# A hybrid attention, convolution and PEER layer: another layout of the gate matrix in memory, five row buffers, and three moved steps

## The chip, the cores and the metric

The kernel runs on one core of a Trainium2 chip, in one launch. The metric is the device time of that core in microseconds, taken as the median of several executions. The core has four engines that compute: TensorE (PE, with its weight loads shown as PEld), VectorE (DVE), ScalarE (ACT) and GpSimd (POOL). SyncE (SP) issues most of the DMAs, ACT and POOL issue some, and each engine works through its own instructions in the order in which they were laid down.

## The reference

One decoder layer on 512 tokens of width 1024. The first half (projections, sparse attention, convolution, output projection) ends at about 360 us and is not touched. The second half is a PEER layer over 16,384 single-neuron experts, with 8 heads that pick 16 experts each:

```
q = (hf @ w_q).reshape(T, PEER_HEADS, 2, 128)
s = einsum('thcd,hcnd->thcn', q, sub_keys)
s1, i1 = top_k(s[:, :, 0], 16);  s2, i2 = top_k(s[:, :, 1], 16)
cand = s1[..., :, None] + s2[..., None, :]        # 256 candidates a head
top_s, pos = top_k(cand, 16);  e_idx = take(cand_idx, pos);  gw = softmax(top_s)
act = gelu(einsum('td,thkd->thk', hc, u_tab[e_idx]))
out = einsum('thk,thkd->td', gw * act, v_tab[e_idx])
```

The result is scaled by a vector and added to the first half's output.

## The kernel before, in words

For the first 384 tokens (TD) the kernel does not gather rows: it multiplies them with all experts, in 128 tiles (NTILE) of 128 experts. The last 128 tokens are done by gathers instead: POOL fetches a U or V row for each token and pick (256 steps in all), and DVE multiplies and sums them.

**U tiles.** `u_split(i)` (line 1056) makes sure that the rows of the next tiles are on their way (`ld()`, line 1051, 512 KB each, four buffers shared by U and V rows), casts tile i to a high part on ACT and takes the low part on DVE. `u_mm` runs 24 matmuls of 384 columns (lines 1070 to 1072), and `u_evac` applies Gelu on ACT. The first eight tiles stay on chip, later ones are written to a spill area by a DMA that ACT issues, until V has begun.

**Routing.** The loop that ends at line 1044 projects one head after another; picking the best 16 is DVE's work and is put in a queue, of which `run(9.0)` takes a part per head. The candidates of each group of 128 tokens follow later, in the loop from line 1206.

**Gate matrix.** `w_chunk` and `w_mm` build, for 16 tokens at a time, the dense matrix of gate weights over all experts: comparisons on DVE, 64 short matmuls on PE, copies on ACT. Each of the 24 blocks of 16 tokens is written to a matrix `wd` in memory by a DMA that ACT issues at line 1138, 1 MB each. V reads it back in groups of eight expert tiles (`w_load`, line 1233; 1.5 MB, issued by SP, 17 loads).

**V tiles.** `v_prep(n)` (line 1286) loads the gate group where a new one begins, loads V rows ahead (line 1301), multiplies gates and Gelu outputs into `g` on DVE, and splits rows and `g` into high and low parts. `v_mm` runs 18 matmuls of 512 columns (lines 1326 to 1328). From about 915 to 1240 us one U tile and one V tile alternate, after that V runs alone. Gather steps are set between the tiles in a fixed proportion.

**Order.** A planner orders PE, ACT, SP and POOL by program order and readiness; from line 1194 on DVE's instructions run in the order of the program. So a DVE step that waits holds all that are written behind it. SP and ACT issue their DMAs in their one instruction stream too: where an issue is held, everything behind it waits.

Of the kernel before, what the change touches and what calls it, by code (L numbers as in the profile page):

```python
# [9 lines left out]
F32 = mybir.dt.float32  # L10
# [10 lines left out]
P = 128  # L21
S = 512
D = 1024
NT = S // P
ND = D // P
H = 8
NCMP = 32
HK = 128
NTILE = 128
TD = 384  # L30
# [78 lines left out]
def layer(ctx: ExitStack, tc: tile.TileContext, a, out):  # L109
    nc = tc.nc  # L110
    mult, add, sub = ALU.mult, ALU.add, ALU.subtract

    def tt(o, i0, i1, op):
        return nc.vector.tensor_tensor(out=o, in0=i0, in1=i1, op=op)  # L114
# [4 lines left out]
    def split(pool_hi, pool_lo, src, shape, tag, bufs=1):  # L119
        hi = pool_hi.tile(shape, F32R, name=tag + "hi", bufs=bufs)  # L120
        lo = pool_lo.tile(shape, F32R, name=tag + "lo", bufs=bufs)
        nc.scalar.copy(hi, src)  # L122
        tt(lo, src, hi.bitcast(F32), sub)
        return hi, lo

    const = ctx.enter_context(tc.tile_pool(name="const", bufs=1, side="left"))
    dram = ctx.enter_context(tc.tile_pool(name="dram", bufs=1, space=DRAM))
    x1d = dram.tile([S, D], F32, name="x1d")
    wd = dram.tile([P, TD // 16, NTILE, 16], F32, name="wd")

    cst = const.tile([P, C_N], F32, name="cst")
    ident = cst[:, C_ID:C_ID + P]
# [12 lines left out]
    with ExitStack() as pre:  # L145
# [630 lines left out]
        for i in range(N + 2):  # L776
            n, pr = i // 4, i % 4
# [132 lines left out]
        gw3 = h2p.tile([P, H, 16], F32, name="gw3")  # L910
        e_i = h2p.tile([P, HK], I32, name="e_i")

        ua = ctx.enter_context(tc.tile_pool(name="upA", bufs=1, side="left"))
        rp = rt.enter_context(tc.tile_pool(name="rpool", bufs=1, side="left"))
# [10 lines left out]
        def run(budget):  # L925
            used = 0.0
            while dq and used < budget:
                cost, f = dq.pop(0)
                f()
                used += cost  # L930
            return used
# [9 lines left out]
        def route_head(t, h, sc):  # L941
            for c in range(2):
                top16(vals[t][:, c, h, :], idxs[t][:, c, h, :], sc[:, t % 2, c, :], P, "s2")
# [5 lines left out]
        def route_items(t):  # L949
# [50 lines left out]
            def soft_b():  # L1000
# [6 lines left out]
            return [(1.6, cands)] + [(0.8, lambda h=h: top(h)) for h in range(H)] + \  # L1007
                [(0.5, soft_a), (2.0, decode), (3.6, lambda: look(0)), (3.6, lambda: look(1)), (0.8, soft_b)]

        wqp = rt0.enter_context(tc.tile_pool(name="wqp", bufs=1, side="right"))  # L1010
        w = wx
        nw[0] = 1
        for h in range(H):
            hi, lo = w
            if h + 1 < H:
                w = wload(a["wq"][h + 1], wqp)
            qs = []
            ps2 = [psQ.tile([P, S], F32, name="mm") for _ in range(2)]
            NS = 2 if h == 0 else 1
            for m in range(NS):  # L1020
                ms_ = slice(m * S // NS, (m + 1) * S // NS)
                for c in range(2):
                    wc = slice(c * P, (c + 1) * P)
                    for d in range(ND):
                        nc.tensor.matmul(ps2[c][:, ms_], hi[:, d, wc], h2hi[:, d, ms_], start=d == 0, stop=False)  # L1025
                        nc.tensor.matmul(ps2[c][:, ms_], hi[:, d, wc], h2lo[:, d, ms_], start=False, stop=False)  # L1026
                        nc.tensor.matmul(ps2[c][:, ms_], lo[:, d, wc], h2hi[:, d, ms_], start=False, stop=d == ND - 1)  # L1027
            for c in range(2):
                ps = ps2[c]
                q = wqk.tile([P, S], F32, name="qs", bufs=2)  # L1030
                nc.scalar.copy(q, ps)
                qs.append(q)
            for t2 in range(2):
                ps = psR.tile([P, 2, 2, P], F32, name="sc")
                for k in range(2):
                    t = 2 * t2 + k
                    for c in range(2):
                        nc.tensor.matmul(ps[:, k, c, :], qs[c][:, t * P:(t + 1) * P], kt[:, 2 * h + c, :],
                                         start=True, stop=True)
                sc = rp.tile([P, 2, 2, P], F32, name="scs", bufs=4)  # L1040
                nc.scalar.copy(sc, ps)
                dq.append((2.2, lambda t=2 * t2, h=h, sc=sc: route_head(t, h, sc)))
                dq.append((2.2, lambda t=2 * t2 + 1, h=h, sc=sc: route_head(t, h, sc)))
            run(9.0)

    up_ = ctx.enter_context(tc.tile_pool(name="upool", bufs=1, side="right"))
    acts = {}
    spill = dram.tile([P, NTILE, TD], F32, name="spill")
    RING = 8

    def ld():
        return ua.tile([P, D], F32, name="ld", bufs=4)

    ust, usp, ue, PU, UB = [], [], [], 2, 3

    def u_split(i):
        if i >= NTILE or i < len(usp):
            return
        while len(ust) < min(i + PU + 1, NTILE):
            ust.append(ld())  # L1060
            nc.sync.dma_start(ust[-1], a["uT"][len(ust) - 1].rearrange("p d e -> p (d e)"))
        src = ust[i].rearrange("p (d e) -> p d e", d=ND)
        usp.append(split(ua, ua, src, [P, ND, P], "u", bufs=UB))

    def u_mm(i, spilled=False):
        u_split(i)
# [21 lines left out]
    flat = lambda z: z.rearrange("p h k -> p (h k)")  # L1088
# [37 lines left out]
    def w_mm(c, q, e1, e2):  # L1126
        if q == 0:
            wbs[c] = wb_.tile([P, NTILE, 16], F32, name="wb", bufs=2)
        wb = wbs[c]
        for g in range(G):  # L1130
            ps = psQ.tile([P, 4, P], F32, name="mm")
            for j in range(4):
                nc.tensor.matmul(ps[:, j, :], e2[:, 4 * g + j, :], e1[:, 0, 2 * g + j // 2, :, j % 2], start=True, stop=False)
                nc.tensor.matmul(ps[:, j, :], e2[:, 4 * g + j, :], e1[:, 1, 2 * g + j // 2, :, j % 2], start=False, stop=True)  # L1134
            tl = q * CH + 4 * g
            act(wb[:, :, tl:tl + 4].rearrange("p i t -> p t i"), ps, AF.Copy, scale=1.0 / GW_SCALE)
        if q == 16 // CH - 1:
            nc.scalar.dma_start(wd[:, c], wb)

    def lists3():  # L1140
        ef = rp.tile([P, HK], F32, name="ef3")
        nc.vector.scalar_tensor_tensor(ef, flat(isel[3][:, 0]), 128.0, flat(isel[3][:, 1]), op0=mult, op1=add)
        nc.vector.tensor_copy(e_i, ef)
        gather_on.append(True)
# [3 lines left out]
    GB, PG = 16, 3  # L1148
# [18 lines left out]
    def gather_step(n):  # L1167
        kind, k = seq[n]
        g = gath(n)
        if kind == "u":  # L1170
            nc.vector.scalar_tensor_tensor(g, g, 1.0, h2n, op0=mult, op1=mult, accum_out=actg[:, k:k + 1])  # L1171
            if k % GB == GB - 1:
                bs = slice(k + 1 - GB, k + 1)
                act(actg[:, bs], actg[:, bs], AF.Gelu)
                tt(actg[:, bs], actg[:, bs], flat(gw3)[:, bs], mult)
        elif k == 0:
            nc.vector.tensor_scalar(acc, g, actg[:, 0:1], None, op0=mult)
        else:
            nc.vector.scalar_tensor_tensor(acc, g, actg[:, k:k + 1], acc, op0=mult, op1=add)  # L1179
# [19 lines left out]
            f()  # L1199
            bud += p - c  # L1200

    for i in range(UB - 1):
        u_split(i)
    while items or pend:
        bud += lead - 1.14
        todo, pend[:] = list(pend), []
# [19 lines left out]
    def group_load(held, k, name, src):  # L1226
        if k not in held:
            held[k] = vp.tile(list(src.shape), F32, name=name, bufs=2)
            nc.sync.dma_start(held[k], src)
            for j in list(held)[:-2]:  # L1230
                del held[j]

    def w_load(k):
        group_load(wts, k, "wt", wd[:, :, k * 8:k * 8 + 8, :])

    def s_load(k):
        group_load(sps, k, "sp", spill[:, k * 4:k * 4 + 4, :])
# [48 lines left out]
    def v_prep(n):  # L1286
        if n >= NTILE:
            return
        i = order[n]
        if n == 0 or i // 8 != order[n - 1] // 8:  # L1290
            w_load(i // 8)
            wseq.pop(0)
        wt = wts[i // 8]
        if i in acts:
            ac = acts.pop(i)
        else:
            if i % 4 == 0:
                s_load(i // 4)
                sseq.pop(0)
            ac = sps[i // 4][:, i % 4, :]  # L1300
        while len(vst) < min(n + 2, NTILE):
            m = order[len(vst)]
            vst.append(ld())
            nc.sync.dma_start(vst[-1], a["vn"][m * P:(m + 1) * P, :])
        if i % 4 == 2 and wseq:
            w_load(wseq[0])
        if i % 4 == 0 and sseq and n + 12 >= order.index(sseq[0] * 4):
            s_load(sseq[0])
        g = vp.tile([P, TD], F32, name="g", bufs=2)
        tt(g.rearrange("p (c t) -> p c t", t=16), wt[:, :, i % 8, :], ac.rearrange("p (c t) -> p c t", t=16), mult)  # L1310
        if n >= NTILE - KL + 2:
            v = split(ua, ua, vst[n].rearrange("p (d e) -> p d e", d=ND), [P, ND, P], "u", bufs=UB)
            v = tuple(z.rearrange("p d e -> p (d e)") for z in v)
        else:
            v = split(vp, vp, vst[n], [P, D], "v", bufs=2)
        gs = split(vp, vp, g, [P, TD], "gs", bufs=KL)
        vsp[n] = gs + v
# [62 lines left out]
```

## Time and profile before

| | |
|---|---|
| three runs | 1612.42, 1619.84, 1621.44 us; median 1619.84 |
| profiled execution | 1614.99 us; span from first to last instruction 1613.2 us |
| PE busy | 1560.4 us (97%) |
| DVE busy | 1293.1 us (80%) |
| ACT busy | 755.2 us (47%) |
| DMA | 416.31 MB, mean 258 GB/s |
| reads of `wd` by SP | 17 of 1536 KB |
| writes of `wd` by ACT | 24 of 1024 KB |
| rows of U, of V | 128 and 128 loads of 512 KB |

Busy shares are means over stages with different limits, so the stages are looked at one by one: U tiles beside routing (461 to 650 us), U tiles beside the gate matrix (650 to 900), U and V in turn (915 to 1225), V alone (to about 1600). The granted clock of TensorE stands in each row of a stretch as a share of full speed: 1.00 is 2.4 GHz, 0.50 is 1.2 GHz.

### The profile page before, as it was taken

The numbers are of one execution on the slowest core, as the hardware profiler recorded it, in microseconds if no ns is written. First come the engines' busy times: TensorE is split into PE (matmuls) and PEld (weight loads), VectorE is DVE, ScalarE is ACT, GpSimd is POOL, SyncE is SP. The second block draws the span as 40 slices with busy tenths as digits, with TensorE's granted clock in tenths as the row PEclk, the third lists the DMA queues.
The fourth block names the chain that finished last, engine by engine and source line by source line (L and its number), as shares of the span: only waits on it lengthen the run. The fifth ranks groups of instructions, "written<-read, shape, count | busy, mean of one in ns | idle before, by whom it ended". The sixth has DMA issues, their size and how long they took to land.

```text
span 1613.2 us, 24117 instructions
## 1 busy us (share of the span) xinstructions
PE 1560.4 (97%) x9033; PEld 1361.8 (84%) x9033; DVE 1293.1 (80%) x2590; ACT 755.2 (47%) x1234; POOL 323.3 (20%) x266
## 2 busy tenths in 40 slices
PE   5999998999999999999999999998999999999998
PEld 3779766898889999999999899997897888888887
DVE  4698667578989999988888387786788888878887
ACT  4335558634334544778778433233232333333332
POOL 0000000000002232221222044443454322222210
PEclk9999999999999999999999999999999999999999
DMA  8443242244006877888888989998999999999993
GB/s 316 151 154 123 107 155 79 95 159 152 15 27 206 297 256 252 308 321 311 314 317 283 336 323 337 328 320 312 347 320 346 340 352 352 359 344 350 350 366 143
DMA packets 157166, 416.31 MB, mean 258 GB/s; under 512 B 13036, under 2 KB 76268, under 8 KB 147960
## 3 DMA queue, kind: packets, MB, share of 16 engines
q1 hardware_dynamic: 104048, 236.73, 42.1%
q0 software_dynamic: 36864, 134.23, 23.2%
q10 hardware_dynamic: 16136, 43.79, 7.2%
q8 instruction: 71, 1.16, 0.3%
q14 instruction: 47, 0.39, 0.1%
HBM read 368.25 MB, written 45.88 MB: 257 GB/s over the span
## 4 chain that ended last, share of the span: by engine, by line
PE 71%; DVE 16%; DMA 6%; ACT 4%; issue 3%; SPq 0%; ACTq 0%; DVEq 0%
PE va L1327 8%; PE va L1328 8%; PE va L1326 8%; PE u L1070 7%; PE u L1071 7%; PE u L1072 7%; DVE acc L1179 3%; DVE ulo L114 3%; DVE ldg L1171 3%; DMA ld<-in_uT_dram 3%; DMA ld<-in_vn_dram 2%; ACT vhi L122 2%; PE mm L1026 2%; PE mm L1025 2%; PE mm L1027 2%
## 5 line engine op out<-in xcount | busy, mean ns | idle before, releaser
L1070 PE MATMUL u<-h2hi,uhi 128*128 128x384 f32 x1024 | 350.4, 342 | 7.4 <-ACT act L117 7.2
L1072 PE MATMUL u<-h2hi,ulo 128*128 128x384 f32 x1024 | 346.4, 338 | 4.4 <-DVE ulo L114 4.4
L1071 PE MATMUL u<-h2lo,uhi 128*128 128x384 f32 x1024 | 348.4, 340 | 0.0
L1163 POOL DMA_INDIRECT ldg<-in_un_dram,e_i x128 | 159.8, 1248 | 869.4 <-DVE cand L114 504.6
L1326 PE MATMUL va<-vhi,gshi 128*128 128x512 f32 x756 | 295.9, 392 | 5.3 <-ACT gshi L122 3.4
L1327 PE MATMUL va<-vlo,gshi 128*128 128x512 f32 x756 | 296.7, 393 | 1.6 <-DVE vlo L114 1.5
L1328 PE MATMUL va<-vhi,gslo 128*128 128x512 f32 x756 | 296.4, 392 | 0.0
L114 DVE TENSOR_TENSOR vlo<-ld,vhi 128x1024 fp32r<-128x1024 f32 x126 | 154.3, 1224 | 128.0 <-ACT vhi L122 127.9
L122 ACT CAST vhi<-ld 128x1024 fp32r<-128x1024 f32 x126 | 132.3, 1051 | 229.6 <-issue 164.6
L1163 POOL DMA_INDIRECT ldg<-in_vn_dram,e_i x128 | 161.3, 1260 | 362.8 <-DVE acc L1179 321.6
L1070 PEld LDWEIGHTS u<-h2hi,uhi 128*128 128x128 f32 x1024 | 194.5, 190 | 10.4 <-ACT act L117 8.3
L122 ACT CAST uhi<-ld 128x1024 fp32r<-128x1024 f32 x130 | 137.7, 1060 | 133.4 <-PE u L1071 86.2
L1072 PEld LDWEIGHTS u<-h2hi,ulo 128*128 128x128 f32 x1024 | 194.2, 190 | 5.0 <-DVE ulo L114 5.0
L1071 PEld LDWEIGHTS u<-h2lo,uhi 128*128 128x128 f32 x1024 | 194.5, 190 | 1.3
L114 DVE TENSOR_TENSOR ulo<-ld,uhi 128x1024 fp32r<-128x1024 f32 x130 | 158.5, 1221 | 27.7 <-ACT uhi L122 26.3
L1326 PEld LDWEIGHTS va<-vhi,gshi 128*128 128x128 f32 x756 | 142.8, 189 | 35.6 <-ACT gshi L122 3.7
L1327 PEld LDWEIGHTS va<-vlo,gshi 128*128 128x128 f32 x756 | 142.7, 189 | 31.9 <-DVE vlo L114 3.0
L1328 PEld LDWEIGHTS va<-vhi,gslo 128*128 128x128 f32 x756 | 142.7, 189 | 30.7 <-DVE gslo L114 0.9
L1179 DVE SCALAR_TENSOR_TENSOR acc<-ldg,actg,acc 128x1024 f32<-128x1024 f32 x127 | 162.5, 1279 | 0.0
L1171 DVE SCALAR_TENSOR_TENSOR ldg<-ldg,h2n 128x1024 f32<-128x1024 f32 x128 | 155.9, 1218 | 0.0
L122 ACT CAST gshi<-g 128x384 fp32r<-128x384 f32 x128 | 65.1, 509 | 156.7 <-DVE g L114 156.6
L117 ACT ACTIVATE wb<-mm 128x512 f32<-128x512 f32 x96 | 96.1, 1110 | 47.2 <-PE mm L1134 47.1
(317 smaller groups left out, 2502.8 us busy)
## 6 DMA issues: line engine op xcount, KB each, us to landing
ld<-in_uT_dram SPq DMA_DIRECT2D x128, 512.0 KB
ld<-in_vn_dram SPq DMA_DIRECT2D x128, 512.0 KB
wt<-wd SPq DMA_DIRECT2D x17, 1536.0 KB
wst<-in_wada_dram SPq DMA_DIRECT2D x24, 1024.0 KB
wd<-wb ACTq DMA_DIRECT2D x24, 1024.0 KB
spill<-actw ACTq DMA_DIRECT2D x84, 192.0 KB
sp<-spill SPq DMA_DIRECT2D x21, 768.0 KB
wst<-in_win_dram SPq DMA_DIRECT2D x9, 1024.0 KB
```

The source lines that it names most:

```text
L114: return nc.vector.tensor_tensor(out=o, in0=i0, in1=i1, op=op)
L117: return nc.scalar.activation(o, i, f, **k)
L122: nc.scalar.copy(hi, src)
L1070: nc.tensor.matmul(ps, hi[:, d, :], h2hi[:, d, :TD], start=d == 0, stop=False)
L1071: nc.tensor.matmul(ps, hi[:, d, :], h2lo[:, d, :TD], start=False, stop=False)
L1072: nc.tensor.matmul(ps, lo[:, d, :], h2hi[:, d, :TD], start=False, stop=d == ND - 1)
L1163: nc.gpsimd.indirect_dma_start(out=gst[-1], out_offset=None, in_=a["un" if kind == "u" else "vn"], in_offset=bass.IndirectOffsetOnAxis(ap= ...
L1171: nc.vector.scalar_tensor_tensor(g, g, 1.0, h2n, op0=mult, op1=mult, accum_out=actg[:, k:k + 1])
L1179: nc.vector.scalar_tensor_tensor(acc, g, actg[:, k:k + 1], acc, op0=mult, op1=add)
L1326: nc.tensor.matmul(vac[t][k], ghi[:, ts_], vhi[:, ks], start=f, stop=False)
L1327: nc.tensor.matmul(vac[t][k], ghi[:, ts_], vlo[:, ks], start=False, stop=False)
L1328: nc.tensor.matmul(vac[t][k], glo[:, ts_], vhi[:, ks], start=False, stop=l)
```

## The change

The matrix `wd` in memory gets another order of its axes: per partition first the 16 groups of eight expert tiles, then the 24 blocks of 16 tokens. Writing a block now puts 16 pieces of 512 bytes per partition at 16 places, where it was one piece of 8 KB; reading a group takes one piece of 12 KB per partition, where it was 24 pieces of 512 bytes. The row buffers are five, and V rows are asked for three ahead of the tile in work, where it was two. The first two `u_split` calls stand inside the loop over heads, in the last head ahead of `run(9.0)`. The product of Gelu outputs and gates of a batch of 16 gathers is moved from the end of the batch's last U step to the start of its first V step, one U step later. The index row of the gathers uses the tile `tmp` of the decode.

```
-    wd = dram.tile([P, TD // 16, NTILE, 16], F32, name="wd")
+    wd = dram.tile([P, NTILE // 8, TD // 16, 8, 16], F32, name="wd")
...
+            return ua.tile([P, D], F32, name="ld", bufs=5)
...
+            if h == H - 1:
+                for i in range(UB - 1):
+                    u_split(i)
             run(9.0)
...
-        return ua.tile([P, D], F32, name="ld", bufs=4)
...
-            nc.scalar.dma_start(wd[:, c], wb)
+            nc.scalar.dma_start(wd[:, :, c], wb.rearrange("p (k i) t -> p k i t", i=8))
...
-        ef = rp.tile([P, HK], F32, name="ef3")
+        ef = flat(rp.tile([P, H, 16], F32, name="tmp"))
...
                 act(actg[:, bs], actg[:, bs], AF.Gelu)
-                tt(actg[:, bs], actg[:, bs], flat(gw3)[:, bs], mult)
-        elif k == 0:
+            return
+        if k % GB == 0:
+            bs = slice(k, k + GB)
+            tt(actg[:, bs], actg[:, bs], flat(gw3)[:, bs], mult)
+        if k == 0:
...
-    for i in range(UB - 1):
-        u_split(i)
...
-        group_load(wts, k, "wt", wd[:, :, k * 8:k * 8 + 8, :])
+        group_load(wts, k, "wt", wd[:, k])
...
-        while len(vst) < min(n + 2, NTILE):
+        while len(vst) < min(n + 3, NTILE):
```

## Rows read from the trace of the kernel before

**Rows 1.** Stretches: us, busy (instructions) PE, PEld, DVE, ACT, POOL, PEclk, DMA, GB/s.
```profile
650.00:900.00 250.00, 249.97 (x1905) 235.24 (x1904) 221.25 (x290) 198.04 (x238) 52.28 (x36) 1.00 0.87 311
...
899.10:911.50 12.40, 12.40 (x73) 12.40 (x73) 3.68 (x3) 4.43 (x6) 0.00 (x0) 1.00 0.84 289
...
918.00:924.80 6.80, 5.49 (x12) 3.94 (x13) 2.16 (x3) 4.59 (x7) 0.00 (x0) 0.50 1.10 338
...
1095.50:1102.30 6.80, 4.35 (x14) 4.35 (x15) 2.18 (x3) 3.63 (x5) 0.00 (x0) 0.50 0.77 308
...
1100.00:1200.00 100.00, 99.19 (x496) 90.09 (x496) 82.20 (x103) 32.86 (x48) 45.14 (x35) 0.99 0.92 322
...
1235.40:1238.80 3.40, 3.40 (x9) 2.64 (x9) 3.40 (x5) 0.51 (x1) 1.93 (x2) 0.50 1.02 406
1240.00:1560.00 320.00, 320.00 (x1413) 264.94 (x1413) 262.93 (x352) 116.16 (x161) 82.64 (x79) 1.00 0.99 351
```

**Rows 2.** Waits of PE, 900 to 1240: us in total, times, longest us.
```profile
PE u L1070 <- ACT act L117: 6.2, 2, 5.3
PE va L1326 <- ACT gshi L122: 3.4, 1, 3.4
PE va L1326 <- ACT vhi L122: 1.9, 2, 1.5
PE va L1327 <- DVE vlo L114: 1.5, 2, 0.8
```

**Rows 3.** Timeline of SP: start us, us, what, times [idle before <-releaser].
```profile
904.62 0.62 SPq L1229 DMA_DIRECT2D wt<-wd  x1
905.36 3.58 SPq L1061 DMA_DIRECT2D ld<-in_uT_dram  x1
...
1076.85 0.53 SPq L1229 DMA_DIRECT2D wt<-wd  x1
1077.99 10.69 SPq L1061 DMA_DIRECT2D ld<-in_uT_dram  x1
...
1557.27 4.88 SPq L1304 DMA_DIRECT2D ld<-in_vn_dram  x2
```

**Rows 4.** Timeline of ACT and of DVE, where they waited between 900 and 1240.
```profile
917.74 1.04 ACT L122 CAST vhi<-ld 128x1024 fp32r<-128x1024 f32 x1 [8.86 <-DMA ld<-in_vn_dram]
...
1096.46 1.04 ACT L122 CAST uhi<-ld 128x1024 fp32r<-128x1024 f32 x1 [11.44 <-DMA ld<-in_uT_dram]
...
1167.55 0.18 DVE L114 TENSOR_TENSOR actg<-actg,gw 128x16 f32<-128x16 f32 x1 [5.42 <-ACT actg L117]
```

**Rows 5.** Timeline of ACT around one write of the gate matrix.
```profile
749.58 0.33 ACTq L1138 DMA_DIRECT2D wd<-wb  x1
...
750.83 0.33 ACTq L1082 DMA_DIRECT2D spill<-actw  x1
752.43 1.99 ACT L117 ACTIVATE wb<-mm 128x512 f32<-128x512 f32 x2 [0.70 <-PE mm L1134]
...
758.01 2.02 ACT L117 ACTIVATE wb<-mm 128x512 f32<-128x512 f32 x2 [1.41 <-PE mm L1134]
```

**Rows 6.** DMA queues, 906 to 909 and 751.0 to 752.5: packets, MB, share.
```profile
q1 hardware_dynamic: 1477, 0.76, 89.6%
...
q10 hardware_dynamic: 73, 0.60, 96.1%
```

**Rows 7.** Waits of SP, 880 to the end: us in total, times, longest.
```profile
SPq L1229 <- DMA wd<-wb: 5.9, 1, 5.9
```

**Rows 8.** Timelines of DVE and PE around the first U tiles.
```profile
374.48 1.22 DVE L114 TENSOR_TENSOR ulo<-ld,uhi 128x1024 fp32r<-128x1024 f32 x1
...
473.51 0.94 DVE L114 TENSOR_TENSOR cand<-vals 128x128 f32<-128x128 f32 x3
...
475.64 0.69 PE L1072 MATMUL u<-h2hi,ulo 128*128 128x384 f32 x1 [3.49 <-DVE ulo L114]
```

**Rows 9.** Waits of DVE over the whole span: us in total, times, longest.
```profile
DVE actg L114 <- ACT actg L117: 7.7, 8, 5.4
```

More of the change, by code (lines that the diff above doesn't have):

```diff
@@ L1008, in route_items, with ld, u_split @@
                 [(0.5, soft_a), (2.0, decode), (3.6, lambda: look(0)), (3.6, lambda: look(1)), (0.8, soft_b)]
+        def ld():
+            return ua.tile([P, D], F32, name="ld", bufs=5)
+        ust, usp, ue, PU, UB = [], [], [], 2, 3
+        def u_split(i):
+            if i >= NTILE or i < len(usp):
+                return
+            while len(ust) < min(i + PU + 1, NTILE):
+                ust.append(ld())
+                nc.sync.dma_start(ust[-1], a["uT"][len(ust) - 1].rearrange("p d e -> p (d e)"))
+            src = ust[i].rearrange("p (d e) -> p d e", d=ND)
+            usp.append(split(ua, ua, src, [P, ND, P], "u", bufs=UB))
         wqp = rt0.enter_context(tc.tile_pool(name="wqp", bufs=1, side="right"))
@@ L1049, in layer @@
     RING = 8
-    def ld():
-        return ua.tile([P, D], F32, name="ld", bufs=4)
[L1054 to L1063, printed above, removed]
     def u_mm(i, spilled=False):
@@ L1174, in gather_step @@
                 act(actg[:, bs], actg[:, bs], AF.Gelu)
-                tt(actg[:, bs], actg[:, bs], flat(gw3)[:, bs], mult)
-        elif k == 0:
+            return
+        if k % GB == 0:
+            bs = slice(k, k + GB)
+            tt(actg[:, bs], actg[:, bs], flat(gw3)[:, bs], mult)
+        if k == 0:
             nc.vector.tensor_scalar(acc, g, actg[:, 0:1], None, op0=mult)
```

## The prediction

> **What bounds the kernel now.** I read the busy shares of the page first, then the table of stretches, the waits of PE, and last the timelines around each wait. The page shows PE at 97% of the span, and the stretches show why a change can only give back small holes: 12.40 us of plain U work start about 71 matmuls, 0.174 us each, and the 320 us of V work after 1240 hold 1413, 0.2265 us each, with PE busy to the last hundredth, at clock 1.00 and with the DMA engines 0.99 busy [rows 1]. Where PE never waits, a DMA saving moves nothing. So the V stage after 1240 has nothing to give, nor has the stage that builds the gate matrix (650 to 900), as long as it keeps its 249.97 of 250 us.
>
> The holes lie where V joins U (915) and where U ends (1217 to 1240). Between 900 and 1240 PE waited 6.2 + 3.4 + 1.9 + 1.5 = 13.0 us [rows 2]. Three waits were followed by a stretch at the lower of the two clock levels (0.50): 12 V matmuls in 5.49 us instead of 12 x 0.2265 = 2.7; 14 U matmuls in 4.35 instead of 2.4; 9 V matmuls in 3.40 instead of 2.0 [rows 1]. That is 2.8 + 1.9 + 1.4 = 6.1 us more. By place, waits and clock together: 6.2 at 915, 7.2 at 1092, 0.9 at 1167, 4.8 at 1225 to 1239; 19.1 us in all.
>
> The cause stands on SP. The load of a gate group takes 0.53 to 0.62 us to issue, but the next issue on SP holds the queue: 3.58 us at 905.36, 10.69 at 1077.99 (the longest), and behind the last of the 17 loads two issues take 4.88, where one behind smaller DMAs takes 0.33 [rows 3, 5]. A gate load is 128 partitions x 24 pieces of 512 bytes, 3072 pieces; a row load is 128. The row loads held up then come late: ACT stood 11.44 us for a U row that SP issued only at 1088.68 or later, and 8.86 us for the first V row [rows 4].
>
> **The change, part by part.**
> *Gate matrix by groups, reading.* A group becomes one piece of 12 KB a partition: 128 pieces instead of 3072, so the hold after 17 loads should go as it is absent after every other 128-piece load. A 512-byte piece took 3 us x 16 x 0.896 / 1477 = 29 ns, an 8 KB piece 1.5 x 16 x 0.961 / 73 = 316 ns [rows 6]; a load costs 16 engines 5.6 us now, an estimate of 3.8 after (39.5 ns per KB), 31 us less over 17 loads, all of it beside a busy PE. What counts is the hold. At 1092 the U row was late by exactly it, so 7.2 of 7.2 go; bounds 0 (something else late at the same time) and 7.2. At 915 two things stay: SP waited 5.9 us for the last gate write before the first gate load [rows 7], and V's first row queues behind that load. I take 4 of 6.2, bounds 0 and 6.2. At 1167 ACT's product of gathers waited behind the late U row; 0.9 of 0.9. At 1225 to 1239 the waits are for V's cast and its low part, partly from DVE still catching up the 5.42 us it lost at 1167.55 [rows 4] and partly from a full DVE order (four gather steps ahead of a V tile); I take half, 2.4, bounds 0 and 4.8.
>
> *Gate matrix by groups, writing.* A write becomes 128 x 16 = 2048 pieces of 512 bytes on ACT's queue, instead of 128 of 8 KB. Engine time: 2048 x 29 / 16 = 3.7 us instead of 128 x 316 / 16 = 2.5; 1.2 us for each of 24 writes, one every 10.4 us, lifts the DMA share of 650 to 900 from 0.87 to about 0.98, no more than the V stage carries without a wait [rows 1]. I cost this at 0; the cover is the U rows' lead of two tiles.
> The hold is the danger. The next issue on ACT is a spill, 1.25 us behind the gate write (749.58, 750.83); behind the spill stand ACT's copies of the gate products, its U casts and the Gelu that frees PE's accumulator. The next copy starts at 752.43 after 0.70 idle, and the one after has 1.41 us of idle ahead of it [rows 5]. So a spill issued by 2.85 us after the gate write moves nothing, and up to 2.85 + 1.41 = 4.3 us is caught up within the two tiles. The trace shows no 2048-piece DMA on ACT; bounds by scaling the pieces 2/3: from the hold that ended 4.3 us after its load (904.62) 2.9 us, from the one that ended 11.8 us after (1076.85) 7.9 us [rows 3]. I take about 3.5 us, nearest to the first, because ACT's queue is empty when the write comes, as SP's was at 904.62: no loss. The upper end costs (7.9 - 4.3) x 24 writes = 86 us.
> The Trainium skill ("DMA: Bandwidth & Descriptors", section "Issuing engines are not separate DMA queues") says that all issuers share the same 16 engines and that where a DMA is issued only saves sequencer time, usually small beside the transfer. The rows above do not agree: sequencer time of 10.69 us stood behind a load of 5.6 us of engine time. By the rule the pieces are as many as before (52,224 read, 49,152 written) and the sum would be 0. The same page ("Specifications") calls 512 bytes enough for line rate; the 29 ns against 316 for 16 times the bytes say 1.5 times dearer, and by the page the 1.2 us per write would be 0.
>
> *Five row buffers, V rows three ahead.* A U and a V tile together take 24 x 0.174 + 18 x 0.2265 = 8.3 us; a V row is now issued two such steps before its cast instead of one. It adds no DMA and no instruction. U's load now waits for the V tile before it, which is cast in the same step; gain and loss alone I bound at -2 and +2 and take 0, since the hold, not the depth, made the rows late.
>
> *First U splits ahead of the last routing heads.* The first low part already ran at 374.48, long before; what PE waited for at 475.64 is the third tile's, which stays in the loop behind the candidates of the last token tile (473.51) [rows 8]. So 0; if the third came earlier too, 3.5 us of wait would go, at most 7 with the slower clock behind it (0.69 us for that matmul); the fifth 512 KB load at the start lies beside a busy PE, at most +1.
>
> *Gather product later.* Eight products leave the place right behind ACT's Gelu, where DVE waited 7.7 us: 5.4 once, counted at 1167, and 2.3 in seven others [rows 9], beside a busy PE. The other edit of the gathers puts their index row into a tile that DVE alone uses; 0.
>
> **Sum.** -7.2 - 4 - 0.9 - 2.4 = -14.5 against the profiled execution's 1614.99 us (span 1613.2): 1600.5. That execution lies 4.9 us below the median of 1619.84, so I add it back: 1605.
>
> **Rivals.**
> *ACT is held by the gate writes (slower).* For: the hold stood behind every 512-byte load, and more traffic runs from 650 to 900 than at 904. Against: 2048 pieces, an empty queue, 2.1 us of idle per two tiles. It decides at a hold ending 4.3 us after the write; it outweighs the gain of 14.5 at 4.3 + 14.5 / 24 = 4.9 us. At 5.5 us it costs 29: 1634; at the bound 86: 1691. Chance 0.17.
> *The holes only change their owner (no change).* DVE works in order, was busy 82.20 of 100 us from 1100 to 1200 [rows 1], and V's low part on it waits for V's cast; if that chain sets 1092 and 1225, only 915 and 1167 shrink: -4.9 or less, 1615. Chance 0.19; it takes in an ACT hold that eats most of the gain.
> *The small pieces only move (no change).* 52,224 pieces are saved in reading and 49,152 added in writing; if a piece costs the kernel the same on either queue, the gain between 900 and 1240 is lost again before 900, and the sum is 0: 1620. Against it: SP's holds meet PE's waits, ACT's would first use up 4.3 us. Chance 0.06. The rule of the page on DMA above would come to this time too.
> *The forecast,* 1597 to 1613: 0.58. A gain at the start as well (-7) lies at its lower edge.
>
> **How the numbers follow.** A measurement of this kernel can tell about 0.5%, 8 us. Faster by more than that, under 1611.7: 0.58; within: 0.25; slower: 0.17. The range 1595 to 1634 holds the forecast, the second rival and the near end of the first; 1597 to 1613 is the forecast's own.
>
> **What would show it.** Right: SP's issue after a gate load takes 0.33 us; the wait of 5.3 us at about 1092 and its half-clock stretch are gone; the spill behind a gate write ends within 4.3 us of it; U tiles between 650 and 900 stay some 5.2 us apart (48 in 250). Wrong: a spill issue of several us with PE waiting on ACT between 650 and 900, or SP free of holds and PE's 13.0 us still there.

## The result, and the profile after

The changed kernel takes 1596.34 us (median; 1595.82 to 1597.10), the kernel before beside it 1618.93 (1612.42 to 1621.44): a ratio of 0.9872, 95% interval [0.9836, 0.9909]. That is faster by 1.3%; the medians alone lie 22.6 us apart, a ratio of 0.9860. The profiled execution took 1596.8 us with a span of 1595.0; before it was 1614.99 and 1613.2.

The page of the changed kernel, busy time and DMA queues (packets, MB, share of 16 engines):

```profile
PE 1550.2 (97%) x9033; PEld 1355.2 (85%) x9033; DVE 1293.0 (81%) x2590; ACT 756.6 (47%) x1234; POOL 323.8 (20%) x266
...
q1 hardware_dynamic: 54000, 236.73, 40.4%
...
q10 hardware_dynamic: 62216, 43.79, 8.8%
```

The same work is done. The small pieces have changed sides: SP's queue q1 held 104,048 packets before, ACT's q10 16,136. Taken as shares of each span, the packets of q1 took 679 us of 16 engines' time before and 644 after, those of q10 116 and 140, those of all queues 1176 and 1168. So 8 us of DMA time went, and 18 us of span. By itself this does not show that the traffic is not the cause, since the small pieces also moved to an earlier stage; the run with the gate loads on ACT, below, tests it.

The stretches of the changed kernel, with the columns of [rows 1] (the last line is of the kernel before, for comparison with the second):

```profile
650.00:900.00 250.00, 247.47 (x1876) 232.34 (x1874) 218.66 (x287) 193.79 (x233) 51.55 (x36) 1.00 0.95 307
900.00:1240.00 340.00, 338.31 (x1703) 306.64 (x1702) 273.49 (x347) 120.79 (x170) 148.12 (x117) 1.00 0.94 347
...
918.00:924.80 6.80, 6.80 (x35) 5.92 (x34) 6.26 (x9) 4.75 (x9) 0.74 (x1) 1.00 1.00 408
1095.50:1102.30 6.80, 6.80 (x37) 6.36 (x36) 5.27 (x7) 1.86 (x3) 3.55 (x3) 1.00 0.93 336
...
1235.40:1238.80 3.40, 3.40 (x17) 2.82 (x16) 3.09 (x5) 0.79 (x3) 0.74 (x1) 1.00 0.81 264
1240.00:1560.00 320.00, 320.00 (x1413) 264.96 (x1413) 262.55 (x349) 114.80 (x159) 75.36 (x73) 1.00 0.95 354
...
900.00:1240.00 340.00, 327.01 (x1614) 294.59 (x1613) 257.60 (x325) 109.53 (x158) 140.54 (x111) 0.97 0.94 328
```

The three stretches that stood at clock 0.50 stand at 1.00 and hold about two to three times as many matmuls (35 for 12, 37 for 14, 17 for 9). From 900 to 1240 the DMA engines are as busy as before, 0.94, while PE starts 89 matmuls more. The V stage holds its 1413 matmuls as before. The one that got worse is the first, in which the gate matrix is built: PE idle 2.5 us of 250 instead of 0.03, and 29 matmuls fewer. (The short gate matmuls among them are 768 in all, 32 for a block of 16 tokens, not the 64 named ahead of the prediction.)

All waits of PE from 900 to 1240, where there were 13.0 us [rows 2]:

```profile
PE u L1073 <- ACT actw L117: 1.7, 1, 1.7
```

SP's timeline at the two places of [rows 3] (with x2, the time runs from the start of the first issue to the end of the second):

```profile
908.41 0.33 SPq L1233 DMA_DIRECT2D wt<-wd  x1
908.84 1.12 SPq L1308 DMA_DIRECT2D ld<-in_vn_dram  x2
...
1067.49 0.33 SPq L1233 DMA_DIRECT2D wt<-wd  x1
1068.62 0.33 SPq L1020 DMA_DIRECT2D ld<-in_uT_dram  x1
```

Behind a gate load stand 0.37 (the first of the two) and 0.33 us where 3.58 and 10.69 stood. All 17 loads show it: the issue behind one took 3.58 to 10.69 us before and takes 0.33 to 0.37 now. What has not gone is SP's wait for the last gate write ahead of the first load [rows 7]; it is 8.3 us, where it was 5.9. The holds have moved to ACT. Its timeline around one of the 24 gate writes, and PE beside it:

```profile
768.11 0.52 ACTq L1141 DMA_DIRECT2D wd<-wb  x1
...
769.35 4.52 ACTq L1085 DMA_DIRECT2D spill<-actw  x1
773.97 1.92 ACT L117 ACTIVATE wb<-mm 128x512 f32<-128x512 f32 x2 [3.72 <-issue]
```

```profile
775.94 0.22 PE L1136 MATMUL mm<-oh,oh 128*128 128x128 f16 x1 [0.50 <-ACT wb L117]
```

The spill behind the write, 0.33 us before [rows 5], holds ACT for 4.52 us here (1.11 to 4.65 over the 24), ACT's copy of the next gate product starts after 3.72 us of idle, where 0.70 stood [rows 5], and PE waits 0.50 us for the accumulator that the copy frees.

For all runs below I read from PE's timeline when three matmuls start: the first of U tile 41 (about where the gate matrix begins), the first of U tile 91 (just ahead of V), and the last of U; tiles count from 0. The time up to tile 41 ran from 643.1 to 649.8 us over thirteen profiles of kernels that hardly differ up to there, so it is left out, and the kernels are compared from there:

| kernel (experiments below) | tile 41 to 91 | 91 to last U | last U to end | sum |
|---|---|---|---|---|
| before | 258.7 | 314.0 | 391.8 | 964.5 |
| after, three profiles | 264.5, 261.2, 263.7 | 298.9, 299.6, 299.8 | 385.3 each | 948.8, 946.2, 948.8 |
| layout alone | 261.6 | 303.6 | 385.5 | 950.7 |
| buffers alone | 258.7 | 306.1 | 390.9 | 955.7 |
| product alone | 258.7 | 312.9 | 391.5 | 963.1 |
| before, gate loads issued by ACT | 268.5 | 301.3 | 389.5 | 959.3 |
| after, four buffers | 263.7 | 301.1 | 385.2 | 950.0 |
| after, spills issued by SP | 261.5 | 301.5 | 385.2 | 948.2 |
| after, gate writes issued by POOL | 257.1 | 303.9 | 385.1 | 946.1 |
| after, gate write behind the next spill, two profiles | 258.9, 258.7 | 300.0, 299.0 | 385.3, 385.6 | 944.3, 943.3 |

(The third profile of after is that of the kernel with the splits put back, whose code from tile 41 on is that of after.)

### The profile page after: what moved, and what is told of

Its sections match the earlier page's. It is cut to its first block, busy times and chain, and to the rows that moved or that the text cites. A ratio compares the mean times of both kernels' runs of the same rounds, so it can differ in the third digit from the quotient of the medians.

```text
span 1595.0 us, 24125 instructions
## 1 busy us (share of the span) xinstructions
PE 1550.2 (97%) x9033; PEld 1355.2 (85%) x9033; DVE 1293.0 (81%) x2590; ACT 756.6 (47%) x1234; POOL 323.8 (20%) x266
## 4 chain that ended last, share of the span: by engine, by line
PE 86%; DVE 5%; ACT 5%; DMA 2%; issue 1%; ACTq 1%; SPq 0%; DVEq 0%
PE va L1332 11%; PE va L1331 11%; PE va L1330 11%; PE u L1073 9%; PE u L1074 9%; PE u L1075 9%; PE mm L1040 2%; PE mm L1039 2%; PE mm L1041 2%; ACT wb L117 2%; PE oT L710 1%; PE mm L294 1%; PE mm L295 1%; PE pt L143 1%; PE mm L296 1%; PE s L663 1%
## 5 line engine op out<-in xcount | busy, mean ns | idle before, releaser
L114 DVE TENSOR_TENSOR vlo<-ld,vhi 128x1024 fp32r<-128x1024 f32 x126 | 154.3, 1225 | 116.0 <-ACT vhi L122 113.8
```

## The experiments

The theory: SP was held behind each gate load by its 3072 small pieces, and this hold made the row loads late. The rivals: the pieces cost by their traffic, whoever issues them; or the depth of the row buffers was the cause. The first four kernels below ran beside the kernel before at 1615.35 us (median), the next four beside 1614.49.

**Layout alone.** The kernel before with the three lines of `wd` changed.

```
-    wd = dram.tile([P, TD // 16, NTILE, 16], F32, name="wd")
+    wd = dram.tile([P, NTILE // 8, TD // 16, 8, 16], F32, name="wd")
-            nc.scalar.dma_start(wd[:, c], wb)
+            nc.scalar.dma_start(wd[:, :, c], wb.rearrange("p (k i) t -> p k i t", i=8))
-        group_load(wts, k, "wt", wd[:, :, k * 8:k * 8 + 8, :])
+        group_load(wts, k, "wt", wd[:, k])
```

> The kernel before with the new order of the gate matrix alone. If the hold of SP behind a gate load of 3072 small pieces made the waits (the theory), this alone gives nearly all: 13 to 22 us less than before, SP's issues behind a gate load 0.33 us, PE's 13 us of waits between 900 and 1240 gone, and ACT held behind the 24 gate writes with some 6 us lost between 650 and 900. If the five buffers and the third V row ahead are what freed the rows (rival), PE still waits several us near 915 and 1092, and the gain is 5 us or less, or a loss by the 6 us on ACT.

Measured: 1600.23 us, ratio 0.9920 [0.9891, 0.9949]. PE's waits from 900 to 1240:

```profile
PE va L1326 <- ACT gshi L122: 1.9, 1, 1.9
PE va L1327 <- DVE vlo L114: 0.3, 1, 0.3
```

The waits at 1092 and from 1225 on are gone; both that stay are at V's start (919 us). From the last U tile to the end the layout alone has all that the whole change has (385.5 against 385.3, from 391.8). This is the largest part of the gain. The stage that builds the gate matrix lost 2.9 us (261.6 against 258.7), half of the 6 that I had expected.

**Buffers alone.** Five buffers, V rows three ahead, and the index row in `tmp`, on the kernel before.

```
-        return ua.tile([P, D], F32, name="ld", bufs=4)
+        return ua.tile([P, D], F32, name="ld", bufs=5)
-        while len(vst) < min(n + 2, NTILE):
+        while len(vst) < min(n + 3, NTILE):
```

> The kernel before with five row buffers and V rows three ahead alone; the gate matrix stays in its old order. Theory: SP is still held 4 to 11 us behind each gate load, and a U row is issued no earlier than before; V rows gain one step, so 0 to 6 us less. Rival (depth of the buffers): 13 to 22 us less and no waits of PE between 900 and 1240.

Measured: 1608.62 us, ratio 0.9963 [0.9948, 0.9979]. That is small, but it is not the nothing at which the forecast had costed the buffers. PE's waits from 900 to 1240, and SP's and ACT's timelines at V's start:

```profile
PE u L1070 <- ACT act L117: 3.6, 1, 3.6
PE va L1327 <- DVE vlo L114: 1.9, 3, 0.8
PE va L1326 <- ACT vhi L122: 1.9, 2, 1.5
PE va L1326 <- ACT gshi L122: 0.7, 1, 0.7
```

```profile
904.68 0.62 SPq L1229 DMA_DIRECT2D wt<-wd  x1
905.70 4.14 SPq L1304 DMA_DIRECT2D ld<-in_vn_dram  x2
```

```profile
915.99 1.05 ACT L122 CAST vhi<-ld 128x1024 fp32r<-128x1024 f32 x1 [6.17 <-DMA ld<-in_vn_dram]
...
917.35 1.04 ACT L122 CAST vhi<-ld 128x1024 fp32r<-128x1024 f32 x1
```

The hold is as long as ever (of the 4.14 us the first issue takes 3.67), but what stands in it are now two V rows; before it was a U row [rows 3]. V's first row is cast at 915.99 instead of 917.74 [rows 4], the second at 917.35 instead of 924.20. The wait at V's start shrank from 3.4 to 0.7 us, so there the order of the loads counts beside the hold. Matmul by matmul, tiles 91 to 93 became 4.7 us shorter. The wait at 1167 is gone as well. At 1092, 3.6 of 5.3 us stay, and the waits behind the last of U stay whole (3.4 us), which speaks against the depth as the main cause.

**Product alone.** The product of the gathers moved to the first V step of a batch, on the kernel before.

```
-                tt(actg[:, bs], actg[:, bs], flat(gw3)[:, bs], mult)
-        elif k == 0:
+            return
+        if k % GB == 0:
+            bs = slice(k, k + GB)
+            tt(actg[:, bs], actg[:, bs], flat(gw3)[:, bs], mult)
+        if k == 0:
```

> The kernel before with the product of gathers one U step later, alone. Theory: DVE's 5.4 us of wait near 1167 goes, and PE's 0.8 us behind it; 0 to 3 us less. Rival (DVE's order is what was late near 1225): 5 us less or more, PE's waits at 1225 to 1239 gone.

Measured: 1616.77 us, ratio 1.0005 [0.9987, 1.0023]: nothing. The longest waits of PE from 900 to 1240:

```profile
PE u L1070 <- ACT act L117: 6.3, 2, 4.8
PE va L1329 <- ACT gshi L122: 2.5, 1, 2.5
```

One of the two waits on `act` is the second one, 1.53 us at 1163. DVE's wait of 5.42 us for the Gelu [rows 4] went with the product, as expected, but this wait of PE is still there (0.81 us before), and with the layout alone it is gone. The prediction had put it down to the late U row, and that holds; my expectation for this run, that it would go with the product, does not.

**Gate loads issued by ACT.** The kernel before, its old layout, the same 3072 pieces a load, but issued by another engine.

```
-            nc.sync.dma_start(held[k], src)
+            (nc.scalar if name == "wt" else nc.sync).dma_start(held[k], src)
```

> The kernel before with the old order of the gate matrix, its 17 loads issued by ACT instead of SP: the same 3072 pieces of 512 bytes, the same time on the DMA engines, but nothing stands behind them on SP. Theory (the held queue is what costs): SP's issues take 0.33 us, PE's waits near 1092 and 1225 are gone, 10 to 18 us less than before. Rival (the small pieces cost DMA engine time, wherever they are issued): no change within 4 us, the U row near 1092 still late.

Measured: 1606.54 us, ratio 0.9942 [0.9919, 0.9965]. PE's waits from 900 to 1240, and ACT's timeline at V's start:

```profile
PE u L1070 <- ACT actw L117: 9.4, 2, 6.7
PE va L1327 <- DVE vlo L114: 0.8, 1, 0.8
PE va L1326 <- ACT vhi L122: 0.3, 1, 0.3
```

```profile
903.92 0.60 ACTq L1229 DMA_DIRECT2D wt<-wd  x1
...
905.15 10.54 ACTq L1082 DMA_DIRECT2D spill<-actw  x1
915.79 0.49 ACT L117 ACTIVATE actw<-u 128x384 f32<-128x384 f32 x1 [9.73 <-issue]
915.81 0.53 ACTq L1229 DMA_DIRECT2D wt<-wd  x1
916.38 4.82 ACTq L1082 DMA_DIRECT2D spill<-actw  x1
```

This is the run that tells the theories apart. Traffic, pieces and buffers are those of before, and the waits at 1092 and 1167 are gone. Where ACT still had spills to issue behind a gate load, it was held for 10.54 and 4.82 us, its Gelu came after 9.73 us of idle, and PE waited 9.4 us. Later on ACT issues no spills, and no issue on it takes over 0.6 us. A hold costs what is queued behind it. The gain by the medians, 8.8 us, is less than the 10 to 18 expected, because of those 9.4 us. One thing this run does not settle: from the last U tile to the end it gets back 2.3 of the 6.5 us that the layout gives (waits of 0.3 and 0.8 at 1226 and 1228 stay, and 1.6 come at 1580 to 1587). For that stretch the share of the traffic stays open.

**What do ACT's holds cost?** Three kernels take them away from the changed kernel in different ways; a fourth has four buffers again.

Spills issued by SP:

```
-            nc.scalar.dma_start(spill[:, i, :], ac)
+            nc.sync.dma_start(spill[:, i, :], ac)
```

> The changed kernel with the spill writes issued by SP instead of ACT: no DMA stands right behind a gate write on ACT, pieces and bytes stay. Theory (ACT's hold costs the stage its 5.9 us): U tiles 41 to 91 take 258.7 us again as before the change, 264.6 in the changed kernel, and the time is 3 to 6 us under the changed kernel's 1596. Rival (the 512-byte writes cost DMA engine time, share 0.98): the stage stays at 262 to 265 us, the time within 2 us of 1596. A loss is possible if SP, which now waits for each Gelu, issues U rows late.

Measured: 1599.09 us, ratio 0.9906 [0.9890, 0.9923]. ACT is held nowhere, yet the stage takes 261.5 us, inside the range of after, and the time is not under the changed kernel's: neither expectation is met. Set tile by tile beside the kernel before, it loses 1.6 us by tile 47, 0.5 from there to tile 85 and 0.8 behind that; the three profiles of after lose 0.1 to 1.1, 1.9 to 2.2 and 0.5 to 3.5. So in the middle of the stage most of the loss goes with ACT's holds, as the theory has it. What costs 1.6 us at its start, I did not settle. From tile 91 to the last U it takes about 2 us more than after: at 916.9 ACT's Gelu had waited 4.98 us for an earlier spill to land, and PE waited 2.3 us for that Gelu.

The gate write queued behind the next spill instead of ahead of it (and the first `w_load` behind `u_evac`):

```
-            nc.scalar.dma_start(wd[:, :, c], wb.rearrange("p (k i) t -> p k i t", i=8))
+            wlate.append((c, wb))
...
-            nc.scalar.dma_start(spill[:, i, :], ac)
+            sp = nc.scalar.dma_start(spill[:, i, :], ac)
+            while wlate:
+                c, wb = wlate.pop(0)
+                with tc.issue_after(sp.ins):
+                    nc.scalar.dma_start(wd[:, :, c], wb.rearrange("p (k i) t -> p k i t", i=8))
```

> The changed kernel with each gate write queued on ACT right behind the spill that it stood ahead of, so that the next DMA on ACT comes some 4.9 us later instead of 1.25. Theory: holds that end 3.7 to 5.9 us after a write then cost at most 1 us each, which ACT's idle time takes up; U tiles 41 to 91 take 259 to 260 us, the time is 3 to 5 us under 1596. Rival (DMA engine time): 262 to 265 us, no change. The last write comes 1.6 us later, which may show as up to 2 us of wait where V begins.

Measured: 1594.95 us, ratio 0.9885 [0.9867, 0.9904]. ACT's DMA issues around one gate write, and the stretch of the stage with the columns of [rows 1]:

```profile
749.94 0.33 ACTq L1085 DMA_DIRECT2D spill<-actw  x1
750.30 0.69 ACTq L1089 DMA_DIRECT2D wd<-wb  x1
...
754.88 0.33 ACTq L1085 DMA_DIRECT2D spill<-actw  x1
```

```profile
650.00:900.00 250.00, 248.95 (x1903) 237.31 (x1902) 221.44 (x289) 198.46 (x237) 59.32 (x36) 1.00 0.95 312
```

The next DMA on ACT now comes 4.6 us after the write and takes 0.33 us. Issues over 0.6 us on ACT fall from 64.5 us in 25 to 11.0 in 10, and the stage from tile 41 to 91 from 264.5 to 258.9, as before. The DMA share is 0.95, the same as after: the loss went while the traffic stayed, so it was the hold. By whole times 1594.95 is less than 2 us under the changed kernel's 1596.34, and not the 3 to 5 expected.

Gate writes issued by POOL:

```
-            nc.scalar.dma_start(wd[:, :, c], wb.rearrange("p (k i) t -> p k i t", i=8))
+            nc.gpsimd.dma_start(wd[:, :, c], wb.rearrange("p (k i) t -> p k i t", i=8))
```

> The changed kernel with the gate writes issued by POOL, between the gathers. Theory: ACT is held no more, U tiles 41 to 91 take 258.7 to 260 us, 3 to 6 us less than 1596, if POOL makes 2048 pieces while it has little else to do there (0.75 gathers a tile). Rival: POOL is held in ACT's place, gathers come late and DVE, in order, waits for them: slower than the changed kernel by several us between 650 and 900.

Measured: 1596.21 us, ratio 0.9890 [0.9872, 0.9908]. One write on POOL:

```profile
746.84 1.18 POOL L1141 DMA_DIRECT2D wd<-wb  x1 [0.53 <-ACT wb L117]
```

Between 650 and 900 (columns of [rows 1]):

```profile
650.00:900.00 250.00, 249.29 (x1913) 240.50 (x1912) 222.24 (x291) 200.00 (x239) 92.98 (x60) 1.00 0.93 316
```

The stage takes 257.1 us, the shortest of all, with 1913 matmuls in 249.29 us where the kernel before had 1905 in 249.97. But from tile 91 to the last of U it gives back 4 to 5 us, 3.13 of them in one wait of PE at 913.7 on ACT's Gelu, which stood behind a cast that had waited 7.71 us for the first V row. So the end hardly moves, and the 3 to 6 us expected of the whole time did not come.

Four buffers in the changed kernel (the two buffer lines undone):

> The changed kernel with four row buffers and V rows two ahead, as before. Theory (order of the gate matrix makes the gain, depth covers only the start of V): 3 to 5 us more than 1596, with 2 to 3 us of wait for the first V tile as in the run with the layout alone, and nothing near 1092. Rival (depth gives nothing once SP is free, as predicted): within 1 us of 1596.

Measured: 1599.22 us, ratio 0.9910 [0.9893, 0.9927]. From tile 91 to the end it takes 686.3 us against 684.2 to 685.1 of after, so with the new layout the fifth buffer would be worth about 1 to 2 us by this run, where alone it gave 8.8 from tile 41 on. The layout alone, which has four buffers too, takes 689.1 there; kernels with four buffers differ by more than the size in question, so it is known only as 1 to 5 us. PE's waits from 900 to 1240:

```profile
PE va L1330 <- ACT gshi L122: 1.1, 1, 1.1
PE u L1073 <- ACT actw L117: 1.0, 1, 1.0
PE va L1331 <- DVE vlo L114: 0.3, 1, 0.3
```

Its first wait is the one at V's start that the layout alone had too (1.1 us; I had expected 2 to 3). From tile 91 to the end the layout alone gives 16.7 us, the buffers alone 8.8, and both 20.7 to 21.6, so the gains do not add in full. At V's start (tiles 91 to 93) they do: 1.7 and 4.7 alone, 5.5 to 6.4 together. What overlaps lies at 1092 and 1167 and behind the last of U.

**The early splits, and the late write once more.** These three ran beside one another on one chip, against 1616.18 us of the kernel before. First the changed kernel itself:

> The changed kernel once more, on the same chip as the next two, so that they can be compared with it. Both theories: 1596 us, 0.987 to 0.990 of the kernel before, and again no stretch of PE waits at 1092 and 1225.

Measured: 1597.59 us, ratio 0.9893 [0.9865, 0.9920], and PE does not wait at 1092 or 1225. Then with the first two U splits back in their old place:

```
-            if h == H - 1:
-                for i in range(UB - 1):
-                    u_split(i)
             run(9.0)
...
+    for i in range(UB - 1):
+        u_split(i)
     while items or pend:
```

> The changed kernel with only the first two U splits put back behind the last routing head. Theory A (these splits ran long before they were needed, and what PE waits for at about 470 us is the third tile's low part): no difference, 1596 us, within 0.2% of the changed kernel, and the wait of 3.49 us is there again. Theory B (the 2.5 us that the changed kernel was ahead at the forty-first U tile came from the early splits): 2 to 3 us slower than the changed kernel, 1599 us, with the forty-first U tile at 648 us or later.

Measured: 1596.20 us, ratio 0.9889 [0.9862, 0.9917]: no difference. The wait at the third tile is in this kernel's trace as in the others (PE from 460 to 480):

```profile
PE u L1072 <- DVE ulo L114: 3.5, 1, 3.5
```

Tile 41 came at 643.1 us, the earliest of all profiles, though theory B wanted 648 or later. So the 2.5 us by which the first profile of after was ahead there are not the early splits; they are scatter between executions. And the late write:

> The changed kernel with every gate write queued behind the next spill instead of ahead of it, as in the earlier run, now beside the changed kernel on one chip. Theory A (the 5 to 6 us that the stage from 650 to 910 us lost are ACT's holds): 3 to 5 us faster than the changed kernel, 1592 us, with the stage from the forty-first to the ninety-first U tile at 259 us. Theory B (the holds lie beside other work and the stage's loss moves the end little): within 1 us of the changed kernel.

Measured: 1593.89 us, ratio 0.9870 [0.9840, 0.9901]; 3.7 us under the changed kernel by the medians, with intervals that overlap. By whole times the late write is not shown to be faster. By the stretch it acts on, both of its profiles (258.9, 258.7) lie under all three of after (261.2 to 264.5). It has the lowest medians I measured, and I would keep it.

## Why the prediction was right, and where its sizes were off

1605 us was forecast and 1596.34 came: within the range of 1595 to 1634, but only 1.3 us from its lower end and 0.7 us below the forecast's own of 1597 to 1613. The mechanism held; several terms were too small. That the total came this near is in part luck: the gains were 7.1 us larger than forecast, and a cost of up to 5.8 us, put in as nothing, took most of that back.

**The hold behind a gate load: right.** It is gone from SP, and with it the waits at 1092 and 1167. The run with the gate loads on ACT shows for these two that it was the issue queue, not the traffic. The DMA time itself came near what I had worked out: 35 us less for reading (31 forecast), 24 more for writing (29), and a DMA share of 0.95 from 650 to 900 (0.98).

**1092, 915 and 1167: sum close, one term too small.** I took 7.2 + 4 + 0.9 = 12.1 us; from tile 91 to the last of U the kernel became 314.0 - 298.9 = 15.1 us shorter, slightly more than the 14.3 that I had found there in all. By place it is 7.6 at 1092, 6.4 at 915 and 1.0 at 1167, so the term at 915 is the one too small. There I let 2.2 of 6.2 us stay, because V's first row queues behind the gate load. It does, but the load holds nothing now, and the fifth buffer puts V's rows ahead of the next U row.

**1225 to 1239: mis-sized.** I took half of 4.8 us, for fear of DVE's full order. From the last U tile to the end 391.8 became 385.3: 6.5 us. Set side by side, the V matmuls behind the last of U show the whole gain by 1239. The full DVE order did not matter once rows came in time, and the holes had cost 1.7 us more than the waits and the one half-clock stretch that I counted.

**Gate writes: zero in the sum, 2.5 to 5.8 us measured.** I expected ACT's hold to end about 3.5 us after the write, and harm only from 4.3 on. The first issue behind the write ended 2.7 to 5.9 us after it (7.8 behind the last, whose spill started only 4.8 us behind it), with a median of 3.9; 9 of 24 passed 4.3, by 13.2 us together. The estimate was near the median, but the mean is 4.3, and one value under a threshold does not say that nothing passes it. PE lost less than half of those 13.2 us. My own signs say so too: of those for "right", the spill within 4.3 us failed in 9 cases, and tiles came 5.3 us apart instead of 5.2; the first of those for "wrong" appeared in small, with spill issues of up to 4.65 us and PE waiting 2.1 us on ACT's copies. This is the first rival's mechanism, at a fifth or less of the 29 us that I had worked out for it.

**Five buffers: zero in the sum;** alone worth 8.8 us from tile 41 on (6.7 by whole times), beyond my bound of 2, with the layout 1 to 5. I judged the depth by rows in the steady stage and overlooked that it changes the order of the first loads at V's start. **Product and early splits: zero, as costed.**

**A premise that was too strong.** I held that a stage in which PE is never idle has nothing to give. The run with the writes on POOL did the stage of the gate matrix in 257.1 us against 258.7, so a PE that shows as busy need not be at its fastest. Why, the runs do not show.

**The other rivals.** "The holes only change their owner" was wrong: between 915 and 1240 nothing stands in their place. (The one wait left from 900 on, 1.7 us at 902, belongs to the gate writes: ACT's Gelu was late behind a held spill.) "The pieces only move" was right about the pieces and wrong about the time: a piece's price depends on what waits behind its issue. The rule that where a DMA is issued saves only the sequencer's time, which is usually small (the Trainium skill, "DMA: Bandwidth & Descriptors", section "Issuing engines are not separate DMA queues"), is not borne out in its "usually small": a held issue took 10.69 us of SP's time behind a load of an estimated 5.6 us of engine time, and on ACT instead of SP the same loads gave a ratio of 0.9942.

**The step back to the median.** On the profiled execution's own terms 1600.5 was forecast and 1596.8 came. The 4.9 us that I added back then took the number further off. The executions of before scatter over 9 us (1612.42 to 1621.44), the four of after first measured over 1.3 and six later ones over 5.2. The kernel before had medians of 1614.49 to 1616.18 beside the experiments, so its profiled 1614.99 was nearer to the usual than the 1619.84 that I went back to.

In all, 15.1 + 6.5 - 5.8 + 2.5 makes the 18.2 us of span that went, but for rounding; the last term is the scatter ahead of tile 41.

## What to carry to other kernels

A DMA of thousands of small pieces costs little by its bytes and much by what is queued behind it on the engine that issues it: look for the long issue right behind it, and see whose work it delays. Such pieces belong where the next DMA of that engine comes late or never, behind the urgent one and not ahead of it. Two edits that cure some of the same waits do not add up in full, and a fear of a new hold is priced by the share of cases above the slack, not by the mean.

## What was not expected of the hardware

The issue of the piecewise DMA itself is short (0.53 to 1.34 us on SP before, 0.52 to 0.60 on ACT after, 1.2 on POOL); the DMA behind it on the same engine pays. Another engine does not: while SP was held from 905.36 to 908.94, ACT issued a spill at 906.29 in 0.33 us. The hold is not a fixed price: the same 3072 pieces held the next issue 3.58 to 10.69 us on SP, 10.54 and 4.82 on ACT; 2048 pieces held ACT from 1.11 to 4.65 us. On POOL the next DMA came 1.5 us or more behind the write and took 1.0 to 1.9 us, where a gather took 0.9 or 1.7 in the changed kernel; PE waited 0.7 us in that stage. A spill that followed 3.3 to 7 us behind the write took 0.33 us in 19 of 24 cases. What the held issue waits for, and what sets the length of a hold, the runs do not show.
